# A hybrid decoder layer whose large SBUF tiles are moved to multiples of 128 bytes

## The chip, the cores and the metric

The kernel runs on one core of a Trainium2 chip. A core has a matrix engine (TensorE, PE in the profile), a vector engine (VectorE, DVE), an activation engine (ScalarE, ACT), GpSimd (POOL) and SyncE (SP), which here only issues DMAs. All of them work out of SBUF, a memory of 128 partitions; a tile takes the same bytes in each partition, so its place is one byte offset. Matrix products land in PSUM. The metric is the device time of one execution in microseconds (us), lower is better.

## The reference: what is computed

One decoder layer over 512 tokens of width 1024, all in float32:

```python
h = rms_norm(x, pre_mix_norm)
mix = hybrid_mixer(h, w_in, ...)            # RG-LRU 256 ch | gated linear attention 256 | MoBA attention 512
x = x + rms_norm(mix @ w_out, post_mix_norm)
h = rms_norm(x, pre_ffn_norm)
f = (silu(h @ w_ffn_gate) * (h @ w_ffn_up)) @ w_ffn_down      # 1024 -> 2816 -> 1024
x = x + rms_norm(f, post_ffn_norm)

# hybrid_mixer
proj = h @ w_in                             # 1024 -> 2832 columns, split into ten parts
y_lru  = rg_lru_branch(...)                 # conv4, gated linear recurrence, times gelu gate
y_gla  = gla_chunked(...)                   # chunks of 64, 4 heads, normed, times silu gate
y_moba = moba_attention(...)                # 8 heads of 64, blocks of 256, T5 bias, softmax
```

The five weight matrices are 1024 x 2832, 1024 x 1024, 1024 x 2816 twice and 2816 x 1024. Nearly all arithmetic is in the products with them.

## The kernel before, in words

**Products.** Every large product is split for precision. An operand `a` becomes `hi`, its value rounded to the type `float32r`, and `lo = a - hi`; the product is `hi*hi + hi*lo + lo*hi`, three matmuls into one PSUM bank (`mm3`, lines 269 to 272, and the same pattern in lines 299 and 1016). A matmul has a stationary operand of 128 x 128 (loaded first, PEld in the profile) and a moving operand of 128 rows by 128 to 512 columns, which streams past it. `hi` is written by ACT and `lo` by DVE (lines 135 and 136; for the FFN lines 944 and 952).

**Stages.** (1) x and the first weights are loaded, x is normalised, transposed and split into `hH`, `hL` (to about 29 us). (2) The projections by `w_in` run on PE with the recurrence, the linear attention and the softmax attention woven between them by an order written out in the program; then the product with `w_out` and the two norms (to about 265 us). (3) The FFN's gate and up products: the first 256 columns as plain products with the moving operands `h2H`, `h2L`, each in two halves of 256 tokens, then ten rounds of a Strassen-like scheme (line 1016), each of seven units of 24 matmuls with 256 moving columns. Four units (A11, A12, S4, A22) move `h2H` and `h2L`; three (S2, S1, S3) move `tH` and `tL`. The stationary operands are the split weights `whi`, `wlo`. (4) The down product, 22 row blocks by 4 token blocks by 2 halves by 3 matmuls, with the split weights `whi`, `wlo` as moving operand of 512 columns, and the last norm.

**What sets the order.** PE's program is written in the order in which it is to run (`manual_schedule`, line 341); other engines follow the program's order and their semaphores. Weights come through the pool `wraw`, loads issued by SyncE, up to four ahead.

**Where tiles lie.** SBUF is filled by pools from two ends. `const`, `wraw`, `whl`, `small` and the pools marked `side="left"` go up from the low end, those marked `side="right"` go down from the high end. Each tile takes its size rounded up to 32 bytes. The constants at the low end are:

```python
331:    make_identity(nc, ident)                  # 512 bytes per partition
332:    mhalf = const.tile([128, 16], F32)        # 64 bytes: exponent -0.5 for the power on POOL
335:    vcol = const.tile([128, NV], F32)         # NV = 19: 76 bytes, so 96
```

`mhalf` is read by POOL's power operations (lines 226, 258 and 378), `vcol` holds small vectors (biases, convolution weights) as columns.

Of the kernel before, what the change touches and what calls it, by code (L numbers as in the profile page):

```python
# [10 lines left out]
F32 = mybir.dt.float32  # L11
# [93 lines left out]
def tile_hybrid_layer(ctx: ExitStack, tc: tile.TileContext,  # L105
# [4 lines left out]
    V = nc.vector  # L110
    pool = lambda **k: ctx.enter_context(tc.tile_pool(**k))
    const = pool(name="const", bufs=1)
# [9 lines left out]
    def bank(tag):  # L122
        return psum.tile([128, 512], F32, name=tag, tag=tag)
# [93 lines left out]
    htp = tc.alloc_tile_pool(name="htp", bufs=1, side="left")  # L217
    hH = htp.tile([128, DC, S], F32R, name="hH")
    hL = htp.tile([128, DC, S], F32R, name="hL")
    sp = tc.alloc_tile_pool(name="startp", bufs=2, side="right")  # L220

    def rstd_of(ss, n, width):
# [106 lines left out]

    ident = const.tile([128, 128], F32)  # L330
    make_identity(nc, ident)
    mhalf = const.tile([128, 16], F32)
    nc.gpsimd.memset(mhalf, -0.5)
    NV = 19
    vcol = const.tile([128, NV], F32)
    vecs = {}

    def vec(name, j):
# [102 lines left out]
    nc.sync.dma_start(gw2, gate_w2[0])  # L441
    pv = bank("at")
    nc.tensor.transpose(pv[:, :NV], vrow, ident[:NV, :NV])
    V.tensor_copy(vcol, pv[:, :NV])

    gp = tc.alloc_tile_pool(name="gp", bufs=1, side="right")

# [681 lines left out]
    sump.release()  # L1129
    rawp.release()  # L1130
    ringp.release()


_INS = ['x', 'pre_mix_norm', 'post_mix_norm', 'pre_ffn_norm', 'post_ffn_norm', 'w_in', 'w_out',
# [23 lines left out]
```

## Time and profile before

| what | value |
|---|---|
| median of 3 runs (range) | 602.11 us (601.75 to 602.14) |
| the profiled execution: its own time | 604.18 us |
| its span (first to last instruction) | 602.2 us |
| mean granted clock of TensorE | 0.98 |
| PE, DVE, ACT, POOL busy | 96%, 68%, 50%, 7% |
| bytes moved by DMA | 68.45 MB, mean 114 GB/s |

The profile is of one execution. A matmul's own duration in it covers its way through the array and overlaps the next one, so how fast matmuls follow each other is read from their start times, not from their durations. [...]

### The profile page before, as it was taken

The page shows a single profiled execution, that of the slowest core. Times are in us where ns is not written, and L with a number is a line of the kernel's source. Part 1 is how long each engine was busy: PE and PEld are TensorE (multiplying, and loading weights), DVE is VectorE, ACT ScalarE, POOL GpSimd, SP SyncE. Part 2 cuts the span into 40 slices and gives each one's busy share as a digit, 9 for nine tenths or more (in the row PEclk, how much of TensorE's full clock was granted, in tenths as well). Part 3 has the DMA queues.
Part 4 walks back from the last instruction along what each step waited for, and adds up shares of the span by engine and source line. Part 5 has one row for each costly group of instructions (what it writes and reads, how often), then busy time and mean ns, then how long its engine had stood idle before and what let it go on. Part 6 is the DMA issues. An engine that isn't in the chain of part 4 may idle for free.

```text
span 602.2 us, 9161 instructions
## 1 busy us (share of the span) xinstructions
PE 575.9 (96%) x3554; PEld 509.2 (85%) x3554; DVE 407.3 (68%) x670; ACT 302.2 (50%) x498; POOL 43.4 (7%) x93
## 2 busy tenths in 40 slices
PE   6999898999898999979999999999999999999995
PEld 5977676888687887879999999999999988888874
DVE  5787386478888845798888788888788533323344
ACT  4656472366788935735455545545554423222231
POOL 3450001201010002010000000000000000000000
PEclk7999988999999999989999999999999999999998
DMA  8456615332322173741234323432314462332002
GB/s 307 127 143 92 147 39 139 89 114 70 97 88 71 52 260 144 220 128 37 71 106 141 106 71 106 140 109 79 112 54 146 155 251 78 106 104 83 23 36 104
DMA packets 67353, 68.45 MB, mean 114 GB/s; under 512 B 4467, under 2 KB 56726, under 8 KB 67310
## 3 DMA queue, kind: packets, MB, share of 16 engines
q1 hardware_dynamic: 66222, 65.24, 34.9%
q0 software_dynamic: 1088, 2.62, 3.0%
q8 instruction: 28, 0.46, 0.3%
q14 instruction: 15, 0.12, 0.1%
HBM read 59.99 MB, written 5.76 MB: 109 GB/s over the span
## 4 chain that ended last, share of the span: by engine, by line
PE 74%; DVE 9%; DMA 7%; ACT 5%; issue 3%; POOL 0%; SPq 0%; DVEq 0%; POOLq 0%; ACTq 0%
PE mm L1016 28%; PE mm L270 7%; PE mm L272 7%; PE mm L271 7%; DMA wraw<-in_w_in_dram 6%; PE mm L299 5%; PE at L1016 5%; PE at L270 4%; PE at L271 4%; PE at L272 4%; DVE wlo L136 3%; DMA wraw<-in_w_ffn_up_dram 1%; DVE h L384 1%; PE at L768 1%; DVE kz L687 1%
## 5 line engine op out<-in xcount | busy, mean ns | idle before, releaser
L136 DVE TENSOR_TENSOR wlo<-wraw,whi 128x512 fp32r<-128x512 f32 (+2 forms) x88 | 70.2, 820 | 53.7 <-ACT whi L135 53.6
L135 ACT ACTIVATE whi<-wraw 128x512 fp32r<-128x512 f32 (+3 forms) x92 | 63.4, 721 | 68.9 <-PE mm L272 29.6
L1016 PE MATMUL mm<-tH,wlo 128*128 128x256 f32 x240 | 67.9, 283 | 0.0
L1016 PE MATMUL mm<-tH,whi 128*128 128x256 f32 x240 | 67.8, 283 | 0.0
L1016 PE MATMUL mm<-tL,whi 128*128 128x256 f32 x240 | 67.8, 282 | 0.0
L1016 PE MATMUL mm<-h2H,whi 128*128 128x256 f32 x240 | 66.3, 276 | 0.0
L1016 PE MATMUL mm<-h2L,whi 128*128 128x256 f32 x240 | 66.3, 276 | 0.0
L1016 PE MATMUL mm<-h2H,wlo 128*128 128x256 f32 x240 | 66.3, 276 | 0.0
L944 ACT ACTIVATE whi<-sum 128x1024 fp32r<-128x1024 f32 x40 | 42.3, 1056 | 34.1 <-DVE sum L920 18.0
L270 PE MATMUL mm<-hH,whi 128*128 128x512 f32 x128 | 53.9, 421 | 0.0
L272 PE MATMUL mm<-hH,wlo 128*128 128x512 f32 x128 | 50.5, 394 | 0.0
L271 PE MATMUL mm<-hL,whi 128*128 128x512 f32 x128 | 50.4, 394 | 0.0
L952 DVE TENSOR_TENSOR wlo<-sum,whi 128x1024 fp32r<-128x1024 f32 x40 | 47.9, 1217 | 0.2 <-ACT whi L944 0.2
L1016 PEld LDWEIGHTS mm<-tH,wlo 128*128 128x128 f32 x240 | 46.0, 192 | 0.0
L1016 PEld LDWEIGHTS mm<-tH,whi 128*128 128x128 f32 x240 | 46.0, 191 | 0.0
L1016 PEld LDWEIGHTS mm<-tL,whi 128*128 128x128 f32 x240 | 46.0, 191 | 0.0
L1016 PEld LDWEIGHTS mm<-h2H,whi 128*128 128x128 f32 x240 | 45.1, 188 | 0.0
L1016 PEld LDWEIGHTS mm<-h2L,whi 128*128 128x128 f32 x240 | 45.1, 188 | 0.0
L1016 PEld LDWEIGHTS mm<-h2H,wlo 128*128 128x128 f32 x240 | 45.1, 188 | 0.0
L136 DVE TENSOR_TENSOR wlo<-aF,whi 128x1024 fp32r<-128x1024 f32 x11 | 13.4, 1224 | 35.9 <-ACT whi L135 35.9
L952 DVE TENSOR_TENSOR wlo<-wraw,whi 128x1024 fp32r<-128x1024 f32 x30 | 36.4, 1217 | 0.0
L272 PE MATMUL mm<-whi,wlo 128*128 128x512 f32 x88 | 34.4, 390 | 0.4 <-DVE wlo L136 0.4
(245 smaller groups left out, 1439.2 us busy)
## 6 DMA issues: line engine op xcount, KB each, us to landing
wraw<-in_w_ffn_down_dram SPq DMA_DIRECT2D x22, 512.0 KB, 3.3
wraw<-in_w_in_dram SPq DMA_DIRECT2D x20, 512.0 KB, 4.1
wraw<-in_w_ffn_gate_dram SPq DMA_DIRECT2D x40, 256.0 KB
wraw<-in_w_ffn_up_dram SPq DMA_DIRECT2D x40, 256.0 KB, 3.5
wraw<-in_w_out_dram SPq DMA_DIRECT2D x8, 512.0 KB, 3.2
x<-in_x_dram SPq DMA_DIRECT2D x4, 512.0 KB, 7.1
xr<-in_x_dram SPq DMA_DIRECT2D x4, 512.0 KB, 5.2
x1d<-xr SPq DMA_DIRECT2D x8, 256.0 KB, 3.3
```

Of the source, the lines that this page charges most:

```text
L135: nc.scalar.activation(hi, t, AF.Copy)
L136: (eng or V).tensor_tensor(out=lo, in0=t, in1=hi.bitcast(F32), op=ALU.subtract)
L270: nc.tensor.matmul(ps, lhsT=lh, rhs=rh, start=start, stop=False)
L271: nc.tensor.matmul(ps, lhsT=lh, rhs=rl, start=False, stop=False)
L272: nc.tensor.matmul(ps, lhsT=ll, rhs=rh, start=False, stop=stop)
L299: nc.tensor.matmul(o, lhsT=lhs[:, cc, ts], rhs=rhs[:, c, :], start=cc == 0 and k == 0, stop=cc == DC - 1 and k == 2)
L384: V.scalar_tensor_tensor(out=h[t][:, cs], in0=xt[t][:, cs], scalar=rstd[t][:, 0:1], in1=gsb[:, cs], op0=ALU.mult, op1=ALU.mult)
L687: V.tensor_tensor(out=kz[j][half(e), e, :], in0=ps[j][half(e), :], in1=ks[half(e), e, :].bitcast(F32), op=ALU.subtract)
L768: nc.tensor.transpose(p[:, (t - kt) * 128:(t - kt + 1) * 128], P[t][:, kt * 128:(kt + 1) * 128], ident)
L944: nc.scalar.activation(hi, src[q, UORD[i]], AF.Copy)
L952: V.tensor_tensor(out=lo, in0=src[q, UORD[i]], in1=hi.bitcast(F32), op=ALU.subtract)
L1016: nc.tensor.matmul(ps, lhsT=a[:, m, c], rhs=b[:, c], start=first and m == c == k == 0, stop=c == 3 and k == 2, skip_group_check=True)
```

## The change

`mhalf` leaves the low end of SBUF: it gets a pool of its own, `edge`, the first on the right side and therefore at the very top, and is widened from 16 to 24 columns (96 bytes). `vcol` is widened from 19 to 32 columns (128 bytes). The one POOL instruction that fills `mhalf` writes 24 columns in place of 16; every other instruction of every engine, its order and what it waits for stay the same.

```diff
@@ -217,6 +217,7 @@
     hL = htp.tile([128, DC, S], F32R, name="hL")
+    edge = tc.alloc_tile_pool(name="edge", bufs=1, side="right")
     sp = tc.alloc_tile_pool(name="startp", bufs=2, side="right")
@@ -329,10 +330,10 @@
-    mhalf = const.tile([128, 16], F32)
+    mhalf = edge.tile([128, 24], F32, name="mhalf")
     nc.gpsimd.memset(mhalf, -0.5)
     NV = 19
-    vcol = const.tile([128, NV], F32)
+    vcol = const.tile([128, 32], F32)
@@ -441,7 +442,7 @@
-    V.tensor_copy(vcol, pv[:, :NV])
+    V.tensor_copy(vcol[:, :NV], pv[:, :NV])
@@ -1129,6 +1130,7 @@
     ringp.release()
+    edge.release()
```

So all tiles behind `vcol` at the low end lie 32 bytes lower, all tiles at the high end 96 bytes lower. Byte offsets, and in brackets what is left of them modulo 128:

| tile | before | after |
|---|---|---|
| `ident` | 16512 (0) | 16512 (0) |
| first `wraw`, `whi`, `wlo` of the weight pools | 17184, 33568, 49952 (32 each) | 17152, 33536, 49920 (0) |
| `mixH`, later `whi` of the second pool (`ringp`) | 69152 (32) | 69120 (0) |
| `tH`, `tL` | 106016, 118304 (32) | 105984, 118272 (0) |
| `hH`, `hL` | 110112, 126496 (32) | 110080, 126464 (0) |
| `h2H`, `h2L` | 196576, 212960 (96) | 196480, 212864 (0) |
| attention: `qs`, `ks`, `kz`, `v2`, `ph`, `pl` | 96 each | 0 each |
| scratch `g` of recurrence and linear attention (ten tiles of 2060 bytes, 2080 apart) | 0, 32, 64, 96 in turn | 0, 32, 64, 96 in turn |
| `brev` (bias table, 8 partitions, rows of 1532 bytes) | 148736 (0) | 148704 (96) |

A slice of `whi` for the projection with 272 columns starts 0, 1088 or 2176 bytes into its tile, so before at 32, 96 and 32 modulo 128; slices of all other large tiles start whole multiples of 512 bytes into theirs.

## Rows read from the trace of the kernel before

**Rows 1.** The page: the span, and each engine's busy us, share and instructions.

```profile
span 602.2 us, 9161 instructions
...
PE 575.9 (96%) x3554; PEld 509.2 (85%) x3554; DVE 407.3 (68%) x670; ACT 302.2 (50%) x498; POOL 43.4 (7%) x93
```

**Rows 2.** The page: the chain that ended last, by engine.

```profile
PE 74%; DVE 9%; DMA 7%; ACT 5%; issue 3%; POOL 0%; SPq 0%; DVEq 0%; POOLq 0%; ACTq 0%
```

**Rows 3.** The chain in the FFN: start us, us, what.

```profile
302.75 2.72 PE at L1016 x24
305.47 16.80 PE mm L1016 x144
```

**Rows 4.** Timeline of PE in a unit that moves tH and tL.

```profile
349.01 0.28 PE L1016 MATMUL mm<-tH,whi 128*128 128x256 f32 x1
...
349.73 0.28 PE L1016 MATMUL mm<-tH,whi 128*128 128x256 f32 x1
```

**Rows 5.** Groups by shape: line, engine, operation, tiles, count | busy, mean ns.

```profile
L1016 PE MATMUL mm<-tH,whi 128*128 128x256 f32 x240 | 67.8, 283 | 0.0
L1016 PE MATMUL mm<-h2H,whi 128*128 128x256 f32 x240 | 66.3, 276 | 0.0
...
L1016 PE MATMUL at<-h2H,whi 128*128 128x256 f32 x80 | 22.1, 276 | 0.0
...
L270 PE MATMUL mm<-h2H,whi 128*128 128x256 f32 x32 | 8.8, 276 | 0.0
...
L270 PE MATMUL mm<-hH,whi 128*128 128x512 f32 x128 | 53.9, 421 | 0.0
...
L270 PE MATMUL mm<-whi 128*128 128x512 f32 x88 | 34.2, 389 | 0.0
...
L270 PE MATMUL mm<-whi,mixH 128*128 128x512 f32 x64 | 25.4, 397 | 0.0
...
L299 PE MATMUL mm<-whi,hH 128*128 128x512 f32 x32 | 13.8, 431 | 0.0
```

**Rows 6.** Stretches: us, busy (instructions) of PE, PEld, DVE, ACT, POOL, clock, DMA.

```profile
476.00:590.00 114.00, 113.63 (x501) 93.79 (x500) 41.25 (x44) 32.09 (x39) 1.08 (x2) 1.00 0.31 106
...
305.47:403.07 97.60, 97.60 (x842) 97.60 (x842) 79.66 (x85) 49.93 (x66) 0.00 (x0) 1.00 0.40 114
100.00:235.00 135.00, 130.09 (x645) 106.78 (x645) 98.20 (x252) 86.50 (x187) 12.82 (x22) 0.99 0.36 113
```

**Rows 7.** Timeline of PE and its stretch (columns as in rows 6) at the lower clock.

```profile
266.58 0.41 PE L272 MATMUL at<-h2H,wlo 128*128 128x256 f32 x1
...
267.86 0.38 PE L272 MATMUL at<-h2H,wlo 128*128 128x256 f32 x1
...
266.00:268.00 2.00, 2.00 (x11) 2.00 (x11) 1.84 (x3) 1.45 (x3) 0.00 (x0) 0.50 0.52 150
```

**Rows 8.** Timeline of PE, products with 272 moving columns, in groups of two.

```profile
20.84 0.41 PE L299 MATMUL mm<-whi,hH 128*128 128x272 f32 x2
...
21.60 0.54 PE L299 MATMUL mm<-whi,hH 128*128 128x272 f32 x3
```

**Rows 9.** The same in groups of three.

```profile
26.60 0.53 PE L299 MATMUL mm<-whi,hH 128*128 128x272 f32 x3
...
27.72 0.41 PE L299 MATMUL mm<-whi,hH 128*128 128x272 f32 x2
```

**Rows 10.** Transposes, timeline and group: moving operand is the identity at offset 0.

```profile
131.04 0.60 PE L768 MATMUL at<-ident,P 128*128 128x128 f32 x4
...
L768 PE MATMUL at<-ident,P 128*128 128x128 f32 x80 | 14.4, 274 | 1.0 <-DVE P L749 1.0
```

**Rows 11.** Stretch at the start; the bias table's DMA; two waits in the timeline.

```profile
5.00:10.00 5.00, 2.22 (x14) 1.58 (x12) 2.96 (x6) 1.89 (x7) 1.28 (x6) 0.87 1.00 360
...
bscr<-brev POOLq DMA_DIRECT2D x1, 1532.0 KB, 33.7
...
69.06 1.15 ACT L135 ACTIVATE whi<-wraw 128x512 fp32r<-128x512 f32 x2 [8.56 <-DMA wraw<-in_w_in_dram]
...
72.98 1.46 PE L606 MATMUL at<-vtok,g 128*128 128x64 f32 x8 [1.83 <-DVE g L599]
```

## The prediction, made before the changed kernel ran

> **What bounds the kernel now.** I read the page first: a span of 602.2 us with PE busy 96% [rows 1]; then the chain that ended last, of which PE is 74% and DVE, ACT and DMA together 21% [rows 2]. No instruction is added, taken away or moved, so the question is whether an instruction's speed depends on where its operands lie, and PE's first.
>
> So I looked at how fast matmuls follow each other. In the chain, an FFN unit that moves h2H and h2L takes 2.72 us for 24 matmuls, 113.3 ns each [rows 3]. The 144 behind it are three units with tH and tL and three with h2: (16.80 - 3 x 2.72) / 72 = 120.0 ns. The timeline says the same: six steps in 0.72 us [rows 4], and the groups, 283 against 276 ns a matmul [rows 5]. Both kinds move 256 columns past the same kind of split weights at clock 1.00; what differs is the tile they move: tH lies at 32 modulo 128, h2H at 96, and elsewhere in SBUF. With 512 columns (down product, `whi` and `wlo` moving, at 32) it is 113.63 / 501 = 226.8 ns [rows 6]. At clock 0.50 256 columns take 1.28 / 6 = 213.3 ns [rows 7], at 1.2 GHz one cycle a column. At 2.4 GHz that would be 106.7 and 213.3 ns. So at the higher clock something gives out: 256 columns take 272 or 288 cycles, 512 take 544.
>
> **A count that fits.** Take 32 cycles at 2.4 GHz (13.3 ns) for each aligned block of 128 bytes that the moving operand touches. 512 columns are 2048 bytes; from offset 32 they touch 17 blocks, 544 cycles: measured 544. 256 columns from 32 touch 9, 288 cycles: tH, measured 288. 272 columns touch 9 from 32 and 10 from 96; the projection moves such slices in groups of two (32, 96) or three (32, 96, 32): 19 blocks, 253.3 ns, and 28 blocks, 373.3 ns. Measured: three groups of two in 0.76 us, 253.3 each [rows 8]; three groups of three in 1.12 us, 373.3 each [rows 9]. Four rows fit one constant. One doesn't: h2 from 96 touches 9 blocks too, but runs in 272 cycles, 8.5 blocks. I have no reason for it, and it keeps my chance for the count at a half.
>
> [...]
>
> **The change part by part.**
>
> *The two constants.* One POOL fill of 24 columns for 16, long before its first reader, on an engine that is busy 7% [rows 1]: nothing.
>
> *Moving operands at 0.* By the count, 256 columns touch 8 blocks (256 cycles), 512 touch 16 (512), 272 touch 9. Then the next limit shows. The nearest row is that of the transposes: their moving operand, the identity, lies at 0 already, each loads a new stationary operand, and four take 0.60 us, the last of them 0.274: (0.60 - 0.274) / 3 = 109 ns [rows 10], 2.3 above 106.7. I take 109 for 256 columns and 213.3 + 2.3 = 215.6 for 512. With the counts of [rows 5]:
> - tH, tL: 3 x 240 = 720 matmuls, 120.0 to 109: 7.9 us.
> - h2 in the ten rounds: 3 x 240 + 3 x 80 = 960, 113.3 to 109: 4.1 us.
> - h2 in lines 270 to 272: 6 x 32 = 192 by 4.3 ns: 0.8 us.
> - down product: 6 x 88 = 528 by 226.8 - 215.6 = 11.2 ns: 5.9 us.
> - 512 columns before the FFN: 3 x (128 + 64 + 32) = 672 by 11.2 ns: 7.5 us of PE's time. There PE is busy 130.09 of 135 us [rows 6], but DVE and ACT take turns on the chain; I count half, 3.8 (bounds 0 and 7.5).
> - 272 columns: 96 by some 2 ns, left out.
>
> In the FFN PE sets the pace alone: in five rounds DVE is busy 79.66 of 97.60 us [rows 6], 15.9 a round, and a round goes from 19.5 to 168 x 109 ns = 18.3, so DVE would be at 87% and PE is still late. Sum: 7.9 + 4.1 + 0.8 + 5.9 + 3.8 = 22.5 us.
>
> Bounds: with no 2.3 ns left over (1872 matmuls of 256, 1200 of 512: 7.1 us) and all of the stage before the FFN (3.7 more) it is 33.3 us. If placement counts for nothing it is 0, and in the third rival it is below nothing.
>
> *DVE, ACT.* Their places change alike. They have 14% of the chain [rows 2], 84 us; one block fewer in 17 would be 5 us at most. No row tells how a DVE or ACT operation depends on its place, so I take 0, with 0 to 5 gained.
>
> *DMA.* In 5 to 10 us the DMA share is 1.00 [rows 11]; a row of x (4096 bytes) touches 33 blocks before and 32 after, 3% of a load of 10 us, 0.3 us at most; I take 0. The other way goes `brev`: from 0 to 96. Its rows of 1532 bytes touch 12 blocks before and 13 after; 1/12 of its 33.7 us [rows 11] is 2.8 us. A w_in load shares the DMA engines with it, ACT waits for that load for 8.56 us until 69.06, and PE for 1.83 us at 72.98 [rows 11]. [...]
>
> [...]
>
> Against the profiled execution, 604.18 us, this gives 581.7. The median of the runs lies 2.07 below that execution, so I predict 579.6; by the measured ends of its terms this case alone spans 573 to 585.
>
> **The rivals.**
> 1. *The weight loads hold 256 columns at 113.3* (0.18). Each matmul has a new stationary operand, and h2's 113.3 may be the weight loads' pace rather than the moving operand's. tH falls to it (720 x 6.7 = 4.8 us), 512 columns gain 5.9 + 3.8: 14.5 us, 587.6. For it: h2's row, which the count doesn't explain; against it: the transposes' 109 with a load each.
> 2. *Only tH gains* (0.08): 17/16 of a cycle a column is the moving operand's best anywhere, as h2 and the 512 columns agree on it. 4.8 us, 597.3.
> 3. *Same offsets collide* (0.12), the slower side. tH and the split weights both lie at 32 modulo 128, h2 at 96 against weights at 32. If reading both from like offsets costs the 6.7 ns, then after the change all lie alike, tH keeps 120 and h2 goes up to it: (960 + 192) x 6.7 ns = 7.7 us, from the FFN's first product on; 609.8. For it: it explains just the row that the count misses. Against it: the groups of two and three in [rows 8, 9].
> 4. *Placement is nothing* (0.14): tH's pace has another cause, such as its part of SBUF. 602.1.
> 5. *The bias table delays the weights* (0.03) and nothing else happens: + 2.8, 604.9.
>
> **How the numbers follow.** Forecast 0.45, 579.6. The range 571 to 604 takes in the forecast, rivals 1, 2 and 4; outside are 3 and 5 (0.15) and a tail of 0.04 below. A difference under 0.2%, 1.2 us, can't be told from none here. Faster: 0.45 + 0.18 + 0.08 = 0.71; same: 0.14; slower: 0.12 + 0.03 = 0.15.
>
> **What would show it.** In the chain of the FFN, 24 matmuls should take 2.6 us in every unit, with tH and with h2, and 144 should take 15.7; in the stretch of the down product, PE's busy time over its count should be near 216 ns. Weight loads pacing would show as 113 ns in all units beside 216 in the down product; colliding offsets as 120 ns in all units; placement without effect as 113 and 120 as now. The bias table's time to landing should stay near 33.7 us. I am wrong if the 512-column matmuls still take 227 ns: then the blocks are not what costs.

## The result, and the profile after

The changed kernel takes 606.34 us (603.99 to 607.95, 13 runs) against 602.14 (601.41 to 604.29, 13 runs) for the kernel before in the same comparison: a ratio of 1.0061 (95% interval 1.0047 to 1.0074), 0.6% slower. The forecast was 579.6, the range 571 to 604. (Ratios are taken over undisturbed runs, so they need not be the quotient of two medians.) Line numbers of `mm3` and the FFN are one higher than before.

The page after, its span, engines and the chain by engine:

```profile
span 604.6 us, 9161 instructions
...
PE 578.3 (96%) x3554; PEld 512.2 (85%) x3554; DVE 406.9 (67%) x670; ACT 302.6 (50%) x498; POOL 43.4 (7%) x93
...
PE 73%; DVE 11%; DMA 7%; ACT 5%; issue 3%; POOL 0%; SPq 0%; DVEq 0%; POOLq 0%; ACTq 0%
```

The picture is that of [rows 1, 2]: the same instructions, PE at 96%, 2.4 us more of it. The chain in the FFN after (start us, us, what) says where:

```profile
300.87 2.85 PE at L1017 x24
303.72 17.17 PE mm L1017 x144
```

A unit that moves h2 took 2.72 us before [rows 3] and takes 2.85 now, 118.6 ns a matmul. In the piece of 144 the three units with tH take (17.17 - 3 x 2.85) / 72 = 120 ns, as before. The groups by shape say the same:

```profile
L1017 PE MATMUL mm<-tH,whi 128*128 128x256 f32 x240 | 67.8, 283 | 0.0
L1017 PE MATMUL mm<-h2H,whi 128*128 128x256 f32 x240 | 67.6, 282 | 0.0
...
L271 PE MATMUL mm<-whi 128*128 128x512 f32 x88 | 34.2, 389 | 0.0
...
L271 PE MATMUL mm<-whi,mixH 128*128 128x512 f32 x64 | 25.5, 398 | 0.0
```

Against [rows 5], tH stays at 283 ns and `whi` of 512 columns at 389; only h2 moves, from 276 to 282. The stretch of the down product (us, then busy us and instructions of PE, PEld, DVE, ACT, POOL; clock; DMA share, GB/s), and, in the timeline of PE, a group of two products with 272 columns and the group of three that starts three groups of two later:

```profile
478.50:592.50 114.00, 113.63 (x502) 93.77 (x501) 40.96 (x44) 32.07 (x39) 1.08 (x2) 1.00 0.31 106
```

```profile
20.30 0.42 PE L300 MATMUL mm<-whi,hH 128*128 128x272 f32 x2
...
21.06 0.54 PE L300 MATMUL mm<-whi,hH 128*128 128x272 f32 x3
```

113.63 / 502 = 226.4 ns, [rows 6] had 226.8; three groups of two in 0.76 us, as in [rows 8], though by the count they touch one block fewer each. So nothing that was to get faster did, and one thing got slower. A unit with h2 after the change, timeline of PE:

```profile
337.89 0.28 PE L1017 MATMUL mm<-h2H,whi 128*128 128x256 f32 x1
338.01 0.28 PE L1017 MATMUL mm<-h2L,whi 128*128 128x256 f32 x1
...
338.48 0.28 PE L1017 MATMUL mm<-h2H,wlo 128*128 128x256 f32 x1
```

Five steps take 0.59 us, 118 ns each; before, three took 0.34.

Not all of it shows in the total. The h2 matmuls cost 960 x 5.3 = 5.1 us in the ten rounds and up to 192 x 5.3 = 1.0 ahead of them, but the median rose by 4.2. The rest came back ahead of the FFN, and sooner loads are the likely way. DMA issues after (KB each, median us to landing), and two waits in the timelines of ACT and PE:

```profile
wraw<-in_w_in_dram SPq DMA_DIRECT2D x20, 512.0 KB, 3.8
...
wraw<-in_w_ffn_up_dram SPq DMA_DIRECT2D x40, 256.0 KB, 3.3
...
bscr<-brev POOLq DMA_DIRECT2D x1, 1532.0 KB, 35.6
```

```profile
67.75 1.16 ACT L135 ACTIVATE whi<-wraw 128x512 fp32r<-128x512 f32 x2 [7.79 <-DMA wraw<-in_w_in_dram]
...
71.67 1.08 PE L607 MATMUL at<-vtok,g 128*128 128x64 f32 x8 [1.07 <-DVE g L600]
```

The bias table lands 1.9 us later than in [rows 11], yet ACT waits 7.79 us for its weights, not 8.56, and PE 1.07, not 1.83.

### The profile page after: what moved, and what is told of

The parts are those of the page before. It is cut to its first block, busy times and chain, and to the rows that moved or that the text cites. A ratio compares the mean times of both kernels' runs of the same rounds, so it can differ in the third digit from the quotient of the medians.

```text
span 604.6 us, 9161 instructions
## 1 busy us (share of the span) xinstructions
PE 578.3 (96%) x3554; PEld 512.2 (85%) x3554; DVE 406.9 (67%) x670; ACT 302.6 (50%) x498; POOL 43.4 (7%) x93
## 3 DMA queue, kind: packets, MB, share of 16 engines
q0 software_dynamic: 1088, 2.62, 3.2%
HBM read 59.99 MB, written 5.76 MB: 109 GB/s over the span
## 4 chain that ended last, share of the span: by engine, by line
PE 73%; DVE 11%; DMA 7%; ACT 5%; issue 3%; POOL 0%; SPq 0%; DVEq 0%; POOLq 0%; ACTq 0%
PE mm L1017 28%; PE mm L271 6%; PE mm L273 6%; PE mm L272 6%; DMA wraw<-in_w_in_dram 5%; PE at L1017 5%; PE mm L300 4%; PE at L271 4%; PE at L272 4%; PE at L273 4%; DVE wlo L136 3%; DVE h L385 1%; DMA gsb<-in_pre_mix_norm_dram 1%; DVE stt L589 1%; PE at L769 1%
## 5 line engine op out<-in xcount | busy, mean ns | idle before, releaser
L1017 PE MATMUL mm<-h2H,whi 128*128 128x256 f32 x240 | 67.6, 282 | 0.0
L1017 PE MATMUL mm<-h2H,wlo 128*128 128x256 f32 x240 | 67.6, 282 | 0.0
L945 ACT ACTIVATE whi<-wraw 128x1024 fp32r<-128x1024 f32 x30 | 31.6, 1056 | 9.0 <-ACT whi L945 7.9
```

Of the source, the lines that this page charges most:

```text
L945: nc.scalar.activation(hi, src[q, UORD[i]], AF.Copy)
L1017: nc.tensor.matmul(ps, lhsT=a[:, m, c], rhs=b[:, c], start=first and m == c == k == 0, stop=c == 3 and k == 2, skip_group_check=True)
```

## The experiments

Three theories stood at the start. **D**: the distance from the stationary to the moving operand, modulo 256 bytes, sets the pace (h2 went from 192 to 128, tH stayed at 0). **M**: the moving operand's own place does. **R**: the part of SBUF. I use "distance" in this sense below.

**A probe of places.** `m1_places` streams matmuls past weights at four starts, with the moving operand at steps of 16 or 32 bytes:

```diff
+for a, b in ((whi, rh), (whi, rl), (wlo, rh)):
+    nc.tensor.matmul(p[:, :n], lhsT=a[:, ws], rhs=b[:, ms], start=k == 0, stop=k == 47)
```

> A probe that leaves out the whole computation and only streams matrix products: 48 matmuls a case, each past a stationary operand of its own, in the FFN's order (first half of the weights by first half of the input, first by second, second by first). A case is named by the PSUM tile it writes: w is the start of the stationary operand modulo 256 bytes, r is how far the moving operand starts past it modulo 256, n is the columns. Theory D (the distance between the two operands sets the pace): for 256 columns r0 gives 120.0 ns a matmul, r192 gives 113.3 and r128 gives 118.6, each the same for w0, w32, w64 and w96. Theory M (the moving operand's own place sets it): cases with one sum w + r are alike, 32 gives 120.0, 224 gives 113.3, 0 gives 120.0 and 128 gives 118.6; so w0 r192 and w32 r192 differ while w0 r224 and w32 r192 agree. Theory R (the part of SBUF, or the kernel around it): all cases of 256 columns have one pace. The block count of the prediction asks 106.7 ns for w + r = 0 or 128 and 120.0 elsewhere. For 512 columns D, M and R expect 226.7 everywhere; the count asks 213.3 at w0 r0.

Its stretch by tile (PE's busy us and count come second): w32r0, w0r128, w32r192, w96r192, w0r112. The pace is (busy - 0.28) / 47.

```profile
0.00:255.20 255.20, 5.92 (x48) 5.83 (x48) 0.99 0.05 17
...
0.00:255.20 255.20, 5.86 (x48) 5.76 (x48) 0.99 0.05 17
...
0.00:255.20 255.20, 5.82 (x48) 5.73 (x48) 0.99 0.05 17
...
0.00:255.20 255.20, 5.62 (x48) 5.53 (x48) 0.99 0.05 17
...
0.00:255.20 255.20, 5.60 (x48) 5.53 (x48) 0.99 0.05 17
```

So 120.0, 118.7, 117.9, 113.6 and 113.2 ns. Distance 0 has one pace wherever the weights start (5.92 us busy at w64 as at w32), and 128 too (5.86 at w32 and w64 as at w0): that is D. The cases w0r128, w32r96 and w64r64 all have the moving operand at 128 and take 118.7, 120.0 and 117.9 ns, so M falls, and R with it. No case of 256 columns goes under 113.2, none of 512 under 226.7: the block count is gone. Two things don't fit. 192 gave 117.9 at three starts and 113.6 at one, and 160 gave 118.7 at w0 and 117.4 at w32, which D doesn't allow. And 512 columns, for which one pace was expected everywhere, settle by their start times at 226.7 ns at distance 0, 228.8 at 64 and 233.3 at 32 and 96: their pace depends on the distance too.

**The change in halves, and tH moved.** On one chip with the kernel before at 602.25:

```diff
e1_left_only (on the kernel before)
-    vcol = const.tile([128, NV], F32)
+    vcol = const.tile([128, 80], F32)
...
e2_right_only (on the kernel before)
-    mhalf = const.tile([128, 16], F32)
+    mhalf = edge.tile([128, 24], F32, name="mhalf")
+    const.tile([128, 16], F32, name="gap")
... (the pool edge as in the change)
e4_th_apart (on the kernel before)
+    ttp.tile([128, 48], F32, name="gap")
     tH = ttp.tile([128, 3, 4, 256], F32R, name="tH")
```

> Only the left part of the change: the table of small columns is widened to 80 and the constant stays where it was, so the weights, tH and tL start at 0 modulo 256 as after the change, and h2H and h2L stay at 224 as before it. Theory M (moving operand's own place): h2 keeps 113.3 ns, time as before the change, 602, less the 1.5 us or so that the change gains elsewhere if that belongs to the left part. Theory D (distance between moving and stationary operand): the distance of h2 becomes 224, which no trace shows yet; anything from 113.3 to 120, so 600 to 608, and the probe's case r224 has to give the same pace as this kernel's units with h2. tH at distance 0 keeps 120.0 by both.

> Only the right part of the change: the constant goes to the other end with 24 columns and a gap of its old size stays, so h2H and h2L start at 128 modulo 256 as after the change, and the weights, tH and tL stay at 32 as before it. Theory M: h2 takes 118.6 ns, 1152 matmuls by 5.3 = 6.1 us, about 608. Theory D: the distance of h2 becomes 96, which no trace shows yet; anything from 113.3 to 120, so 602 to 610, with the pace of the probe's case r96. tH at distance 0 keeps 120.0 by both.

> The kernel before with a gap of 192 bytes ahead of tH and tL alone: they start at 224 modulo 256, the weights stay at 32, and h2 is as before. Theory D: the distance of tH becomes 192, that of h2 before the change, so its units go from 120.0 to 113.3 ns a matmul: 720 x 6.7 = 4.8 us less, 597.3. Theory M says the same here, as 224 is h2's own place. Theory R (tH is slow because of the part of SBUF that it lies in, or because of what runs beside its units): 120.0 and 602.

The chains in the FFN, of the left part alone, the right part alone, and tH apart:

```profile
280.61 2.84 PE at L1016 x24
283.45 17.16 PE mm L1016 x144
```

```profile
281.61 2.88 PE at L1018 x24
284.49 17.27 PE mm L1018 x144
```

```profile
281.35 2.72 PE at L1017 x24
284.07 16.32 PE mm L1017 x144
```

h2 at a distance of 224 takes 118.3 ns (the probe's 118.3), at 96 it takes 120.0 (120.0). M wanted 113.3 and 118.6. The times are 606.06 (ratio 1.0072, 1.0042 to 1.0102) and 608.89 (1.0111, 1.0086 to 1.0136): each half alone is slower, because each half changes h2's distance. With tH at 192 the 144 take 16.32 us, 113.3 ns throughout, and the time is 597.62 (0.9917, 0.9894 to 0.9940) for the 597.3 that D gave. M says the same for this kernel, but fell above; so tH's 120 ns was a matter of its distance, not of what runs beside it or of the part of SBUF.

**Does one place have one pace?** `m2_order` puts all operand tiles at one place modulo 4096 and varies which case runs ahead (edits to the first probe, and a new list of cases):

```diff
-    whi = big.tile([128, 1088], F32R, name="whi")
+    whi = big.tile([128, 2048], F32R, name="whi")
...
-        p = psum.tile([128, 512], F32, name=f"w{w}r{r}n{n}", tag=f"b{i % 4}")
+        p = psum.tile([128, 512], F32, name=f"r{r}after{prev}x", tag=f"b{i % 4}")
```

> A second probe that leaves out the whole computation: the first probe's stream of 48 matmuls a case with 256 columns, all operand tiles now at one place modulo 4096, stationary operand at 32 modulo 256; a PSUM tile's name says how far the moving operand starts past the stationary one and which case ran just ahead (r192after0: distance 192, behind a case of distance 0). In the kernel a distance of 192 always ran at 113.3 ns a matmul, in the first probe at 117.8 three times and 113.3 once. If the places alone decide and the first probe differed by the 256 bytes between its halves, all cases of 192 give 113.3 here whatever ran ahead. If it is a matter of how the stream starts, the cases of 192 fall into two groups, 113.3 and 117.8, by what ran ahead. If the distance counts modulo 256, then 448 is as 192, 256 as 0, 320 as 64 and 352 as 96; modulo 512 they are free to differ. 0 and 96 should give 120.0, 128 118.6, 224 118.4 as in the kernel and the first probe.

By tile: r192after128, r448after192, r256after448, r96after112, r112after64.

```profile
0.00:358.40 358.40, 5.63 (x48) 5.55 (x48) 0.99 0.03 13
...
0.00:358.40 358.40, 5.60 (x48) 5.51 (x48) 0.99 0.03 13
...
0.00:358.40 358.40, 5.90 (x48) 5.80 (x48) 0.99 0.03 13
...
0.00:358.40 358.40, 5.92 (x48) 5.82 (x48) 0.99 0.03 13
...
0.00:358.40 358.40, 5.60 (x48) 5.52 (x48) 0.99 0.03 13
```

113.8, 113.2, 119.6, 120.0 and 113.2 ns. 448 goes with 192 and 256 with 0, so the distance counts modulo 256. Both fast distances are narrow: 104, 108, 116 and 120 took 119.8 to 121.9 ns, and 176, 184, 188, 196, 200 and 208 took 119.1 to 120.2. All cases of 192 from the second on (the first was mixed with waits for its operands) ran at 113.3 after some six steps, whatever ran ahead; the question seemed closed, and it was not.

**Undoing the loss, keeping the alignment.** On one chip with the kernel before at 602.23:

```diff
e6_h2_apart (on the changed kernel)
-    mhalf = edge.tile([128, 24], F32, name="mhalf")
+    mhalf = edge.tile([128, 72], F32, name="mhalf")
...
e5_both_apart (e6, and)
+    ttp.tile([128, 48], F32, name="gap")
b2_before_again: no edit
```

> The changed kernel with the moved constant made 192 bytes wider, so that h2H and h2L start at 192 modulo 256 and not at 128; the weights, tH and tL stay at 0. Theory D (distance): h2 goes back to 113.3 ns, 1152 x 5.3 = 6.1 us less than the change: 600.3, and the FFN's rounds (199.66 us after the change) take 194.6. If the change's loss came from elsewhere in the aligned layout (the weights, hH or the small tables), 606 stays.

> As the kernel with h2 apart, and 192 bytes ahead of tH and tL too: weights at 0 modulo 256, tH, tL, h2H and h2L all at 192. Theory D: every matmul of 256 columns at 113.3 ns; against the change 6.1 + 720 x 6.7 = 4.8 us less: 595.5, at most the 597.6 of the kernel before with tH apart. If alignment of the weights to 256 bytes has a price or a gain of its own, this differs from that kernel by it; the distance alone says they are equal within 2 us.

> The kernel before, unchanged, for a second profile. The first one was 2 us above the median and lost them at the start of the FFN: PE waited until 8.1 us after the 1184th matmul for the normalised rows, against 6.2 to 7.4 in the four other kernels, and then ran at half clock. If that is one execution's chance, this profile shows the first FFN round starting near 278.5 us, not 280.6; if it belongs to the places of the kernel before, 280.6 comes again.

h2 at 192 gives 600.64 (ratio 0.9978, 0.9962 to 0.9994), both at 192 give 595.80 (0.9891, 0.9857 to 0.9926): 600.3 and 595.5 were expected. With h2 at 192 both paces are those of the kernel before, and the time is still 1.6 us below it: that much of the new layout's effect is not the pace. The second profile of the kernel before, chain in the FFN:

```profile
279.67 2.83 PE mm L1016 x24
282.49 2.83 PE at L1016 x24
285.32 16.81 PE mm L1016 x144
302.13 2.72 PE at L1016 x24
```

The first round starts at 279.67, between the two that were expected, in an execution of 603.52 us; the first profile had 280.51 in one of 604.18. Less what each lies above its median, both give 278.4 to 278.5, which speaks for chance. The surprise is the first two units: 2.83 us, 117.9 ns, at the places where the first profile has 2.72 from the start. Behind the first tH units it is 2.72 again. One place, two paces.

**Loads, and whether the second pace can last.** `m3_loads` times weight loads one by one at eight starts; the two kernels with everything at 192 run again, unedited.

```diff
+d = t[:, off // 4:off // 4 + 1024].rearrange("p (c n) -> p c n", c=8)
+nc.sync.dma_start(d, w_in[:, rep * 128:rep * 128 + 128].rearrange("(c p) n -> p c n", p=128))
```

> A probe that leaves out the whole computation and only loads weights, one DMA after the other: 512 KB in pieces of 512 bytes (as w_in is loaded) and 512 KB in rows of 4096 bytes (as w_ffn_down is), six times each at eight starts modulo 256 in SBUF; a tile's name says the start and the kind. In the eight profiles so far the loads of w_in took 3.8 us from issue to landing where the weight buffers start at 0 modulo 256 and 4.1 where they start at 32, those of w_ffn_up 3.3 against 3.5, and those in rows of 4096 bytes 3.3 at either. If the start in SBUF does it, pieces land some 0.2 to 0.3 us sooner at 0 than at 32 here too, and rows show less than 0.1; the other starts are open (64 and 128 like 0, or like 32). If something else in the four aligned kernels did it, all starts give one time, within 0.1 us.

> The kernel with weights at 0 and both tH, tL and h2 at 192, timed again. Two things are to be told. Against the kernel before with tH apart alone (weights at 32), the same pace everywhere: if the sooner loads are worth the 1 to 1.5 us that the stage before the FFN shows in the aligned kernels, this one is 1 to 1.5 us under the other; if not, equal. And at a distance of 192 a second pace was seen, 117.8 ns, from the FFN's start until the first unit with tH. Where all distances are 192 nothing breaks it: an execution that starts so would stay there, 1872 x 4.4 = 8 us longer, near 604. If some execution lies there the second pace lasts; if all lie within 594 to 598 it is left again, or not entered.

> The kernel before with tH and tL 192 bytes further, timed again beside the one with weights at 0: 597.6 if its loads land later, 596 to 596.5 if the place of the weight buffers is worth nothing; near 605 in an execution that keeps the second pace.

DMA issues of the probe:

```profile
at0pieces<-in_w_in_dram SPq DMA_DIRECT2D x6, 512.0 KB, 3.4
at0rows<-in_w_ffn_down_dram SPq DMA_DIRECT2D x6, 512.0 KB, 3.3
...
at32pieces<-in_w_in_dram SPq DMA_DIRECT2D x6, 512.0 KB, 3.6
...
at224pieces<-in_w_in_dram SPq DMA_DIRECT2D x6, 512.0 KB, 3.7
```

Pieces of 512 bytes land 0.2 us sooner at 0 than at 32; 96 has 3.5, the other starts 3.6 or 3.7; rows of 4096 bytes show no such order (3.1 to 3.3). In the kernels the loads of w_ffn_up keep to it (3.3 us in all six profiles with weights at 0, 3.5 in all five with weights at 32), those of w_in not quite: 3.8 in all six, but 4.1, 4.1, 4.2, 4.1 and 3.8 in the five. So a start at 0 is the fastest for pieces, and why is not shown: 128, a whole block of the prediction's count, has 3.6 as 32 has, and 96 has 3.5.

The two medians are 596.64 (ratio 0.9874, 0.9855 to 0.9893) with weights at 0 and 598.25 (0.9955, 0.9925 to 0.9985) with weights at 32. The two ratios are not to be compared: three long executions count in the second, and the one of 603.81 does not in the first. Of 24 executions of the two kernels with all distances at 192 (eight with weights at 0, sixteen with weights at 32), twenty took 594.07 to 599.30 us and four took 603.81, 604.36, 605.20 and 605.71. Without the four the medians are 595.61 and 597.75, the weights at 0 sooner by 2.1. The four lie 6.6 to 8.2 us above: the size of a stream that stays at 117.8 (1872 x 4.4 = 8.2). The clock isn't what makes them long: their mean granted clock is 0.986 to 0.992, that of the others 0.981 to 0.995. No profile fell on one of these four, so the link to the second pace is argued from the size.

**Does the start pick the pace, and has 112 two?** `m4_pauses` lets each case start behind a pause at the half clock (its mean clock is 0.795, that of the other two probes of matmuls 0.99); `e8_both_112` takes the changed kernel and uses each pair of tiles from byte 112 on.

```diff
m4_pauses
+nc.scalar.activation(rh[:, 3064:3072], dly[:, :8], AF.Copy)
...
+nc.tensor.matmul(p[:, 256:264], lhsT=whi[:, :128], rhs=rh[:, 3064:3072], start=True, stop=True)
...
e8_both_112 (on the changed kernel; tH and tL likewise)
-    h2H = h2p.tile([128, DC, S], F32R, name="h2H")
-    h2L = h2p.tile([128, DC, S], F32R, name="h2L")
+    h2 = h2p.tile([128, 2 * DC * S + 32], F32R, name="h2")[:, 28:28 + 2 * DC * S]
+    h2H, h2L = (h2[:, k * DC * S:(k + 1) * DC * S].rearrange("p (c s) -> p c s", c=DC) for k in range(2))
```

> A third probe that leaves out the whole computation: 120 matmuls of 256 columns a case at a distance of 192, 112 or 0, each case behind a pause of PE (a letter in the tile's name, d to k, from some 5 us to 13 us, in which ScalarE copies), so that each starts at the half clock and rises to the full one in its course, as the FFN's first products do behind the wait for the normalised rows. Two paces at one place: of the eight cases of 192 some go on at 113.3 ns and some at 117.8 after the rise, as the kernel did (five profiles at 113.3 from there, one at 117.8). One pace: all eight at 113.3, and then the 117.8 in the kernel's profile has another cause. For 112 the second probe had 113.3 to 113.5 in all seven cases but never rose from the half clock there; if it too has two paces, some of the eight show it. For 0, 120.0 in all.

> The changed kernel with tH and tL, and h2H and h2L, each pair in one tile that starts at 0 modulo 256 and is used from byte 112 on; weights at 0. The map of the probes carried to the kernel: at a distance of 112 all 1872 matmuls take 113.3 ns, so 595.8, the time of the kernel with both at 192. If 112 has no second pace, all its executions lie within 593.5 to 599 and none near 604; if it has one as 192 has, about one in five lies near 604. If the block of 128 bytes that the prediction counted has any part, a start at 112, which adds no block but lies off every multiple of 32, would show nothing in particular; and if a start off the multiples of 32 is dear in itself for the engines that write these tiles, DVE and ACT operations on them get longer and the stage before the FFN with them.

Timeline of PE in the probe, after the rise, in three cases:

```profile
116.80 0.28 PE L58 MATMUL r192pausee<-rh,wlo 128*128 128x256 f32 x1
...
120.88 0.28 PE L58 MATMUL r192pausee<-rh,wlo 128*128 128x256 f32 x1
...
427.80 0.28 PE L58 MATMUL r192pausei<-rh,whi 128*128 128x256 f32 x1
...
431.81 0.28 PE L58 MATMUL r192pausei<-rl,whi 128*128 128x256 f32 x1
...
454.80 0.28 PE L58 MATMUL r112pausei<-rh,whi 128*128 128x256 f32 x1
...
458.88 0.28 PE L58 MATMUL r112pausei<-rh,whi 128*128 128x256 f32 x1
```

36 steps in 4.08 us, 34 in 4.01, 36 in 4.08: 113.3, 117.9 and 113.3 ns. Of the eight cases of 192, five went on at 113.3 and three at 117.8; of 112 all eight went on at 113.3 (seven of them after six to twelve slower steps), of 0 all eight at 120.0. Each case kept its pace to its end. A start out of the half clock is not needed for the slower one: the three cases of the first probe at 117.9 began at the full clock, and what picks the pace there is not known. The kernel at 112 takes 594.95 (593.90 to 596.90, six executions), ratio 0.9874 (0.9851 to 0.9896): the lowest median, though not told apart from both at 192, and none of the six is long. Six are few: at four in 24, six without one come up a third of the time, so one pace at 112 is likely from the probes and not shown by the kernel. Starts off the multiples of 32 cost DVE and ACT nothing: 407.2 and 302.2 us busy, as with both at 192. Its chain in the FFN:

```profile
279.45 2.72 PE at L1017 x24
282.17 16.32 PE mm L1017 x144
```

**Does the load of the stationary operand take part?** The last probe narrows it, so that less is loaded beside the stream:

```diff
-                    ws = slice(q + (4 * h + c) * 128, q + (4 * h + c) * 128 + 128)
+                    ws = slice(q + (4 * h + c) * 128, q + (4 * h + c) * 128 + n)
```

> A fourth probe that leaves out the whole computation: the second probe's stream (48 matmuls of 256 columns a case, stationary operand at 32 modulo 256), now with stationary operands of 128, 64 and 32 columns at seven distances each, and 128 once more at the end; a tile's name says the distance and the width. If the pace is set by the load of the next stationary operand reading SBUF beside the moving operand, a load of 32 columns reads a quarter and the pace hardly depends on the distance: all distances within 2 ns of each other, at 113.3 or below. If the moving operand's reads alone set it, the width changes nothing: 120.0 at 0 and 96, 118.6 at 128, 118.3 at 224, 113.3 at 112 at every width. Width 128 at both ends must repeat the map of the second probe.

By tile: r0w128, r0w64, r0w32, r64w128, r64w32, r224w32.

```profile
0.00:205.10 205.10, 5.93 (x48) 5.83 (x48) 0.99 0.06 21
...
0.00:205.10 205.10, 5.61 (x48) 5.47 (x48) 0.99 0.06 21
...
0.00:205.10 205.10, 5.61 (x48) 5.18 (x48) 0.99 0.06 21
...
0.00:205.10 205.10, 5.81 (x48) 5.72 (x48) 0.99 0.06 21
...
0.00:205.10 205.10, 5.61 (x48) 5.18 (x48) 0.99 0.06 21
...
0.00:205.10 205.10, 5.80 (x48) 5.19 (x48) 0.99 0.06 21
```

At distance 0 the pace falls from 120 to 113.4 ns when the load is halved; with 32 columns four of the seven distances (0, 64, 112, 192) have 113.2 to 113.8, the others 115.5 to 117.5. So the width of the stationary operand counts: at distance 0 the same moving reads at the same places are faster beside a narrower one. A narrower one also writes fewer partitions of PSUM, and no run separates the two, so that the load's own reading is the reason is argued. Neither expectation holds as written, since some distances stay slow at the smallest width and, at 64 columns, the two fast distances got slower: 192 takes 118.9 ns (5.87 us) and 112 takes 116.6 (5.76). What exactly collides stays open.

## Why the prediction was wrong

**The count that fits** is the step that failed. 13.3 ns for each block of 128 bytes that the moving operand touches gave the terms for tH (7.9 us), h2 (4.1 and 0.8), the down product (5.9) and the 512 columns before the FFN (3.8). Measured: tH 0, the 512 columns 0, h2 minus 5.1 and up to minus 1.0. What set the pace is the distance between the two operands, which the change left alone for tH and altered for h2. The count had one constant, four rows that agreed and one, h2, that didn't. tH and h2 move the same 256 columns, and h2's two operands lay differently to each other than tH's: that pair could have told the count from a matter of two places. That four rows fitted one constant was chance. Its cycles and GHz are an estimate from [rows 7], where 256 columns take 213.3 ns at clock 0.50, 1.2 a ns; the 106.7 ns for clock 1.00 is half of that, and no run came down to it. The groups of 272 columns kept their time, as the distance has it: `whi` and `hH` moved by the same 32 bytes.

**109 ns for 256 columns**, the pace that the sum goes down to, was also misread: the transposes of [rows 10] move 128 columns, so they say nothing of 256, and the 109 that speaks against rival 1 falls too. No run here had 256 columns under 113.2. The lower end of "573 to 585" doesn't follow either: with the prediction's own bound of 33.3 us it is 568.8, and no sum of its terms is given for 585.

**"Wrong if 512 columns still take 227 ns"** is what came: 226.4. That row of the kernel after was enough to end the theory; the probe has 226.7 to 233.3 at four starts, and none lower.

**Rival 3** came nearest: two places, not one, set the pace. But its rule was another. It held that like offsets modulo 128 collide and that h2 would join tH at 120; the price 7.7 us, 609.8. After the change all places are alike modulo 128, yet h2 runs at 118.6 and tH at 120: the distance counts modulo 256, and that of h2 is 128, not 0. By its rule the right part alone (distance 96, unlike offsets) should have cost nothing; it cost 6.6 us. Its price was 1152 x 6.7; measured is 5.1 in the rounds and at most 1.0 ahead of them.

**Loads**, taken as 0, are the likely source of 1 to 2 us that came back. The start of the first FFN round, less what the profiled execution lies above its kernel's median:

| kernel | weights start at | h2, tH apart by | ns, h2 and tH | median us | first round starts at |
|---|---|---|---|---|---|
| before (two profiles) | 32 | 192, 0 | 113.3, 120.0 | 602.1 to 603.0 | 278.5, 278.4 |
| right part alone | 32 | 96, 0 | 120.0, 120.0 | 608.89 | 279.2 |
| tH apart | 32 | 192, 192 | 113.3, 113.3 | 597.62 | 278.8 |
| tH apart, again | 32 | 192, 192 | 113.3, 113.3 | 597.94 without three long ones | 279.0 |
| after | 0 | 128, 0 | 118.6, 120.0 | 606.34 | 277.9 |
| left part alone | 0 | 224, 0 | 118.3, 120.0 | 606.06 | 277.8 |
| h2 apart | 0 | 192, 0 | 113.3, 120.0 | 600.64 | 277.1 |
| both apart | 0 | 192, 192 | 113.3, 113.3 | 595.80 | 276.9 |
| both apart, again | 0 | 192, 192 | 113.3, 113.3 | 595.61 without one long one | 276.7 |
| both at 112 | 0 | 112, 112 | 113.3, 113.3 | 594.95 | 276.2 |

Every kernel whose weight buffers start at 0 is sooner than every one where they start at 32, by 1.7 us in the mean. This rests on the subtraction, which takes an execution's excess to lie ahead of the FFN: as read, the starts overlap (278.63 at the earliest with weights at 32, 278.80 at the latest with weights at 0). The medians agree without it: h2 apart is 1.6 us below the kernel before, and both apart 2.1 below tH apart, each at the same paces. The prediction looked for this in rows of 4096 bytes, which show nothing, and passed over the pieces of 512. In all six profiles with weights at 0 PE's wait of [rows 11] is 1.05 to 1.16 us, in all five with weights at 32 it is 1.73 to 1.88; 0.7 us of the gain goes that way. The way of the rest was not followed, and other tiles moved with the weights, so that the loads are the whole of it isn't shown.

**Rival 5** had the table's delay and not its consequence: the table lands 1.9 us later, where it counted 2.8, but the load behind it is awaited for less time than before. It takes 35.4 to 35.6 us in all six profiles with weights at 0 and 33.7 or 33.8 in the five others; the table's place and that of the weights changed together, so which of the two does it is open.

**The two constants, DVE and ACT**: costed at nothing, and no kernel here speaks against it (DVE 407.3 us busy before and 406.9 after, ACT 302.2 and 302.6). The split of the sum shows why the range missed too: all five of its terms hung on one constant, so they failed together.

## What to carry to other kernels

Where PE is the bound and each matmul loads a new stationary operand (here `float32r` with 256 moving columns), look at where the two operands lie relative to each other, not at whether each is aligned; a gap of 192 bytes in front of one tile was worth 0.8% here, aligning everything cost 0.6%. The good distances are exact: 113.3 ns at 112 and 192, and 119.1 to 121.9 at 4 bytes beside them. Read the pace from start times by tile, and when two tiles differ, move one of them alone before building a formula on absolute places. A fast place can have a second, slower pace, as 192 has with 117.8 ns; time it often enough to see it.

## What the runs showed of the hardware

- Matmuls of 256 columns in `float32r` at clock 1.00 with a new stationary operand of 128 columns each: 113.3 ns at distances 112 and 192, 117.8 at 64, 118.3 at 224, 118.6 at 128, 120.0 at 0 and 96. No run went under 113.2, with narrower stationary operands neither. 4 or 8 bytes beside 112 and 4 to 16 beside 192 it was 119.1 to 121.9. At clock 0.50 it was 213.3 ns at 192 ([rows 7]), and steps of 0.21 us at 96 (`e2_right_only`), 112 (`e8_both_112`) and 224 (`e1_left_only`) just ahead of the FFN's rounds: these four distances show no difference there.
- With 512 columns the probe had 226.7 ns at distance 0, 228.8 at 64, 233.3 at 32 and 96.
- With stationary operands of 64 or 32 columns distance 0 took 113.4 ns in place of 120.0, while at 64 columns 112 took 116.6 and 192 took 118.9.
- At 192 a second pace of 117.8 exists. Three of eight starts out of the half clock took it and kept it for the rest of the case's 120 matmuls; one profile of the kernel before kept it until the first tH unit. That it can last for the whole FFN is argued from the times of four executions and not shown by a profile.
- Loads of 512 KB in pieces of 512 bytes landed in 3.4 us at a start of 0 modulo 256 and in 3.5 to 3.7 elsewhere; in rows of 4096 bytes in 3.1 to 3.3 anywhere.
